# A gated residual block on one core: a third stream of block pairs, operand sums made by transfers, and paced preparation

## The chip, the cores and the metric

One core of a Trainium2 chip runs the kernel. The metric is the device time of one execution in microseconds (us), the median of repeated runs. The engines are TensorE (PE, matrix products), VectorE (DVE), ScalarE (ACT), GpSimd (POOL) and SyncE (SP, which here only issues DMA transfers).

## The reference, cut to what matters

A sequence of S = 512 positions of width D = 1024 goes through one residual block. All matrices are float32.

```python
h = rmsnorm(x, norm_mix_g)
u, v, bg, cg, xs, ga, gb = split(einsum('bsd,dc->bsc', h, w_in))   # seven products 1024 x 1024
u = gelu(u); v = rmsnorm(gelu(v), norm_v_g)
a = spatial_gating(u, v, w_s, b_s)                                # branch A
c = bg * causal_dwconv(cg * xs, conv_w)                           # branch B: three streams bg, cg, xs
m = sigmoid(ga + b_gate_a) * (a @ w_proj_a) + sigmoid(gb + b_gate_b) * (c @ w_proj_b)
x = x + m @ w_out
x = x + relu(rmsnorm(x, norm_ff_g) @ w_ff1) ** 2 @ w_ff2          # 1024 -> 4096 -> 1024
return rmsnorm(x, norm_final_g)
```

## The kernel before

**Products.** Activations stay in SBUF with channels on the 128 partitions and the 512 positions along the row; the weights stream in from HBM, each byte once. To keep float32 accuracy with the faster fp32r matmul, every operand is split into a high part (a cast on ACT, L117, `whi<-raw`) and a low part (a subtraction on DVE, L118, `wlo<-raw,whi`), and every product is three matmuls: high by high, high by low, low by high.

There are two forms of product. A **unit** (`unit_matmuls`, L265 to L267) is one output tile of 128 channels over all 1024 input channels: 8 steps of 3 matmuls of 512 columns. A **block pair** (`block_pair`) makes two such output tiles at once by Strassen's method in Winograd's form: the 2 by 2 blocks are combined by additions, and 7 block products replace 8. One block product (`product`, L283 to L285) is 12 matmuls of 256 columns. The order on PE is P1, P2, then P7 of the pair ahead (kept back in the list `late`), E, P6, then D of the pair ahead, then F. P7 and D of one pair both add into the bank A of that pair, and ACT copies the bank (L313) after P7 and before D may write to it again. `first` and `second` are the functions that turn the two output tiles into the next value.

**Operands.** A pair needs four split operands: `a1` (two blocks), `s31` (two sums of blocks), `s42` (two further sums) and `a22` (one block). The two-block operands rotate through 4 buffers, `a22` has one buffer of its own, which D of the pair ahead must have read first. DVE makes the sums: `add1` (L218, 1024 elements in a row) for s31 and `add2` (L222 and L223, 512 each) for s42.

**Loads.** SP issues one 1 MB transfer for a pair (`raw<-w_pair`, four blocks, L148) or for two units (`raw<-w_main`, L144). There are two raw buffers. The step `load(ld + 2)` stands behind the last split of load `ld`, which for a pair is that of a22, so a load starts when the buffer's last reader on DVE is done.

**Order.** Preparation steps (splits, sums, loads) stand in one list in the order of their use. `pump()` takes one step ahead of every product; `need()` takes steps until the operand at hand is there. The tile framework's scheduler then settles the order on each engine, and each engine runs its own list in that order.

**Stages.** The v product with its own small loads (0 to 31 us of the profiled execution); units of u with the spatial gating `mix` woven in; gate A as 4 pairs with units of the projection of a between them; branch B in four calls of `c_pair`, each two pairs (the streams `c_w` and `x_w`) and then two units (the third stream `b_w`); gate B with its projection; the output projection; and the two feed-forward products, where pairs and units alternate. After `x_first` or `x_second`, `conv` does the three-tap convolution on DVE: the first tap at L616, the others at L618.

## Time and profile before

| | |
|---|---|
| median of 3 runs | 789.09 us (789.01 to 789.1) |
| the profiled execution, its own time | 788.42 us |
| its span in the trace | 786.6 us |
| PE busy in the span | 778.4 us, 99% |
| DVE, ACT, POOL busy | 568.8 us (72%), 365.7 us (46%), 6.3 us (1%) |
| granted TensorE clock, mean | 0.997 |
| moved by DMA | 83.60 MB |

Of the span, the trace gives each instruction's start, its length, and in brackets how long its engine was idle before it and what released it. "whi<-raw" reads as: writes the tile whi from the tile raw. The profiled execution is 0.67 us shorter than the median of the runs, and 1.8 us of it lie outside the span.

### The profile page before, as it was taken

The numbers are of one execution on the slowest core, as the hardware profiler recorded it, in microseconds if no ns is written. First come the engines' busy times: TensorE is split into PE (matmuls) and PEld (weight loads), VectorE is DVE, ScalarE is ACT, GpSimd is POOL, SyncE is SP. The second block draws the span as 40 slices with busy tenths as digits, with TensorE's granted clock in tenths as the row PEclk, the third lists the DMA queues.
The fourth block names the chain that finished last, engine by engine and source line by source line (L and its number), as shares of the span: only waits on it lengthen the run. The fifth ranks groups of instructions, "written<-read, shape, count | busy, mean of one in ns | idle before, by whom it ended". The sixth has DMA issues, their size and how long they took to land.

```text
span 786.6 us, 11560 instructions
## 1 busy us (share of the span) xinstructions
PE 778.4 (99%) x4798; PEld 701.3 (89%) x4798; DVE 568.8 (72%) x854; ACT 365.7 (46%) x548; POOL 6.3 (1%) x14
## 2 busy tenths in 40 slices
PE   9999999999999999999999999999999999999996
PEld 6888899999999999999988999889988999889886
DVE  7849785566889889766769998647955687557644
ACT  8625363444344444444555676324742365226521
POOL 0000000000000000000000000000000000000000
PEclk9999999999999999999999999999999999999998
DMA  9602113331332314332633033330353024311403
GB/s 333 218 40 92 68 55 107 107 107 55 107 115 102 107 62 154 107 108 86 229 114 107 1 107 125 144 107 1 107 182 140 1 91 177 107 54 55 161 1 107
DMA packets 21443, 83.60 MB, mean 106 GB/s; under 512 B 1936, under 2 KB 2960, under 8 KB 17296
## 3 DMA queue, kind: packets, MB, share of 16 engines
q1 hardware_dynamic: 20384, 81.27, 29.5%
q10 hardware_dynamic: 1008, 1.61, 0.6%
q8 instruction: 37, 0.61, 0.3%
q14 instruction: 14, 0.11, 0.0%
HBM read 80.78 MB, written 2.10 MB: 105 GB/s over the span
## 4 chain that ended last, share of the span: by engine, by line
PE 98%; DMA 0%; ACT 0%; DVE 0%; POOLq 0%; DVEq 0%; issue 0%
PE bank L265 17%; PE bank L266 17%; PE bank L267 17%; PE bank L284 14%; PE bank L285 14%; PE bank L283 14%; PE bank L477 6%; PE bank L528 1%; DMA vec<-vecs 0%; PE bank L369 0%; PE st L358 0%; PE bank L747 0%; PE st L793 0%; DVE ob L759 0%; POOLq L929 0%; ACT x L120 0%
## 5 line engine op out<-in xcount | busy, mean ns | idle before, releaser
L117 ACT CAST whi<-raw 128x1024 fp32r<-128x1024 f32 (+1 forms) x136 | 129.0, 950 | 180.4 <-PE bank L266 117.7
L118 DVE TENSOR_TENSOR wlo<-raw,whi 128x1024 fp32r<-128x1024 f32 (+1 forms) x136 | 148.8, 1096 | 18.2 <-ACT whi L117 16.3
L117 ACT CAST whi<-wsum 128x1024 fp32r<-128x1024 f32 x64 | 67.2, 1051 | 80.9 <-PE bank L266 41.3
L265 PE MATMUL bank<-z,whi 128*128 128x512 f32 (+1 forms) x272 | 102.7, 378 | 0.0
L266 PE MATMUL bank<-z,whi 128*128 128x512 f32 (+1 forms) x272 | 102.6, 377 | 0.0
L267 PE MATMUL bank<-z,wlo 128*128 128x512 f32 (+1 forms) x272 | 102.4, 376 | 0.0
L118 DVE TENSOR_TENSOR wlo<-wsum,whi 128x1024 fp32r<-128x1024 f32 x64 | 78.2, 1222 | 21.0 <-ACT whi L117 20.2
L283 PE MATMUL bank<-ft,whi 128*128 128x256 f32 x256 | 72.5, 283 | 0.0
L285 PE MATMUL bank<-xc,wlo 128*128 128x256 f32 x256 | 72.4, 283 | 0.0
L284 PE MATMUL bank<-xc,whi 128*128 128x256 f32 x256 | 72.4, 283 | 0.0
L285 PE MATMUL bank<-ft,wlo 128*128 128x256 f32 x256 | 72.4, 283 | 0.0
L284 PE MATMUL bank<-ft,whi 128*128 128x256 f32 x256 | 72.4, 283 | 0.0
L283 PE MATMUL bank<-xc,whi 128*128 128x256 f32 x256 | 72.3, 282 | 0.0
L860 DVE TENSOR_TENSOR res<-bank,res 128x512 f32<-128x512 f32 x30 | 20.7, 691 | 60.9 <-PE bank L267 60.9
L267 PEld LDWEIGHTS bank<-z,wlo 128*128 128x128 f32 x272 | 51.2, 188 | 9.4
L265 PEld LDWEIGHTS bank<-z,whi 128*128 128x128 f32 x272 | 51.2, 188 | 9.2
L266 PEld LDWEIGHTS bank<-z,whi 128*128 128x128 f32 x272 | 51.2, 188 | 8.9
L284 PE MATMUL bank<-fb,whi 128*128 128x256 f32 x192 | 54.4, 283 | 0.0
L283 PE MATMUL bank<-fb,whi 128*128 128x256 f32 x192 | 54.4, 283 | 0.0
L283 PE MATMUL bank<-x,whi 128*128 128x256 f32 x192 | 54.4, 283 | 0.0
L285 PE MATMUL bank<-x,wlo 128*128 128x256 f32 x192 | 54.3, 283 | 0.0
L284 PE MATMUL bank<-x,whi 128*128 128x256 f32 x192 | 54.3, 283 | 0.0
(157 smaller groups left out, 1797.6 us busy)
## 6 DMA issues: line engine op xcount, KB each, us to landing
raw<-w_main SPq DMA_DIRECT2D x36, 1024.0 KB, 4.9
raw<-w_pair SPq DMA_DIRECT2D x32, 1024.0 KB, 4.8
vraw<-w_v SPq DMA_DIRECT2D x16, 256.0 KB, 5.5
xin<-xT SPq DMA_DIRECT2D x8, 256.0 KB, 5.2
res<-xT SPq DMA_DIRECT2D x8, 256.0 KB, 4.7
out_a<-o SPq DMA_DIRECT2D x4, 256.0 KB, 2.3
wsT<-w_sT ACTq DMA_DIRECT2D x2, 256.0 KB, 4.8
bsb<-b_sb ACTq DMA_DIRECT2D x2, 256.0 KB, 6.0
```

What stands on the lines that cost most here:

```text
L117: nc.scalar.copy(hi, src)
L118: nc.vector.tensor_tensor(lo, src, hi.bitcast(F32), op=ALU.subtract)
L265: nc.tensor.matmul(psum, hi[:, c], act_hi[k][:, cols], start=k == 0, stop=False)
L266: nc.tensor.matmul(psum, hi[:, c], act_lo[k][:, cols], start=False, stop=False)
L267: nc.tensor.matmul(psum, lo[:, c], act_hi[k][:, cols], start=False, stop=k == KT - 1)
L283: nc.tensor.matmul(out, w_hi, x_hi, start=first and sl == 0, stop=False, skip_group_check=True)
L284: nc.tensor.matmul(out, w_hi, x_lo, start=False, stop=False, skip_group_check=True)
L285: nc.tensor.matmul(out, w_lo, x_hi, start=False, stop=sl == KS - 1, skip_group_check=True)
L477: nc.tensor.matmul(vbanks[h][b], xs[k][:, b * P : (b + 1) * P], ws, start=k == 0 and ws is vh and xs is xh, stop=k == KT - 1 and xs is xl,)
L528: nc.tensor.matmul(pm[:, b * P : (b + 1) * P], vt[b][g // 4][:, (g % 4) * P : (g % 4 + 1) * P], wsT[:, g, :], start=True, stop=True,)
L860: nc.vector.tensor_add(res[j], py, res[j])
```

## The change

The third stream of branch B becomes a third block pair in each `c_pair`, with `b_first` and `b_second`; so there are 36 pairs where there were 32, and 32 loads of units where there were 36. The sums of s31 are no longer added on DVE: for each pair, GpSimd issues one transfer that copies two blocks (512 KB, L225 of the new kernel) into a slot, and, when that has landed, one that adds a third block to both (L226, `accum_op`). One such slot exists until the mixing of branch A has ended, three after that. The load of a pair on SP brings three blocks (768 KB) instead of four. The first tap of the convolution goes from DVE to ACT (L649 of the new kernel). `pump()` no longer takes a split whose time, by a model clock `now` that counts products, lies ahead of an assumed landing of its load.

```diff
@@ -135,9 +135,16 @@
     wfree = list(range(N_WBUF))
     a22_busy = [False]
 
+
+
+    now = [0.0]
+    T_PRODUCT, T_HALF, T_RAW, T_SUM = 1.44, 2.72, 7.0, 12.0
+    t_load = {}
+
     def load(n):
         if n >= len(loads) or n in raw_of:
             return
+        t_load[n] = now[0]
         kind, i = loads[n]
         r = raws.tile([P, 4, S], F32, name="raw")
         if kind == "u":
@@ -145,12 +152,12 @@
                 r.rearrange("p (u a) s -> p u (a s)", u=2), w_main[i : i + 2].rearrange("u p f -> p u f")
             )
         else:
-            nc.sync.dma_start(r, w_pair[i])
+            nc.sync.dma_start(r[:, :3, :], w_pair[i, :, :3, :])
         raw_of[n] = r
 
-    def add_operand(src, n=2):
-        o = {"ready": False, "n": n}
+    def add_operand(src, due, n=2):
+
+        o = {"ready": False, "n": n, "due": due}
 
         def step():
             if n == 2:
@@ -181,11 +188,11 @@
 
         while steps and n:
             step, o = steps[0]
-            if o is not None and (not wfree if o["n"] == 2 else a22_busy[0]):
+            if o is not None and ((not wfree if o["n"] == 2 else a22_busy[0]) or o["due"]() > now[0]):
                 return
             steps.pop(0)
             step()
-            n -= 1
+            n -= o is not None
 
     def need(o):
         while not o["ready"]:
@@ -193,16 +200,30 @@
 
     units = []
     pairs = []
+
+    def raw_due(ld):
+        return t_load.get(ld, 1e9) + T_RAW
 
     def plan_units(n):
         for _ in range(n // 2):
             ld = len(loads)
             loads.append(("u", len(units)))
             for e in range(2):
-                units.append(add_operand(lambda ld=ld, e=e: raw_of[ld][:, 2 * e : 2 * e + 2, :]))
+                units.append(add_operand(
+                    lambda ld=ld, e=e: raw_of[ld][:, 2 * e : 2 * e + 2, :], lambda ld=ld: raw_due(ld)
+                ))
             add_step(lambda ld=ld: load(ld + 2))
 
-    sums_t = None
+    s31_free, s31_of, t_build = [], {}, {}
+
+    def build():
+
+        while s31_free and len(t_build) < w_pair.shape[0]:
+            i, s = len(t_build), s31_free.pop(0)
+            s31_of[i] = s
+            t_build[i] = now[0]
+            nc.gpsimd.dma_start(s.t, w_pair[i, :, 1:3, :])
+            nc.gpsimd.dma_start(s.t, w_pair[i, :, 3:4, :].broadcast_to([P, 2, S]), accum_op=ALU.add)
 
     def plan_pair():
         ld = len(loads)
@@ -211,24 +232,28 @@
         def raw(a, b):
             return raw_of[ld][:, a:b, :]
 
-        s31, s42 = sums_t[0].t, sums_t[1].t
-
-        def add1():
-
-            nc.vector.tensor_tensor(s31, raw(1, 3), raw(3, 4).broadcast_to([P, 2, S]), op=ALU.add)
+        n = len(pairs)
+
+        def due():
+            return raw_due(ld)
+
+        def done1():
+            s31_free.append(s31_of.pop(n))
+            build()
 
         def add2():
 
+            s31, s42 = s31_of[n].t, s42_t.t
             nc.vector.tensor_tensor(s42[:, 1, :], s31[:, 1, :], raw(1, 2)[:, 0, :], op=ALU.add)
             nc.vector.tensor_tensor(s42[:, 0, :], s42[:, 1, :], raw(0, 1)[:, 0, :], op=ALU.add)
 
         tl = {}
-        tl["a1"] = add_operand(lambda: raw(0, 2))
-        add_step(add1)
-        tl["s31"] = add_operand(lambda: s31)
+        tl["a1"] = add_operand(lambda: raw(0, 2), due)
+        tl["s31"] = add_operand(lambda: s31_of[n].t, lambda: t_build.get(n, 1e9) + T_SUM)
         add_step(add2)
-        tl["s42"] = add_operand(lambda: s42)
-        tl["a22"] = add_operand(lambda: raw(2, 3), n=1)
+        add_step(done1)
+        tl["s42"] = add_operand(lambda: s42_t.t, due)
+        tl["a22"] = add_operand(lambda: raw(2, 3), due, n=1)
         add_step(lambda: load(ld + 2))
         pairs.append(tl)
 
@@ -255,7 +280,9 @@
                 need(o)
             unit_k(psum, o, k, act_hi, act_lo)
             if k == KT // 2 - 1:
+                now[0] += T_HALF
                 run_late()
+        now[0] += T_HALF
         release(o)
         run_late()
 
@@ -283,6 +310,7 @@
             nc.tensor.matmul(out, w_hi, x_hi, start=first and sl == 0, stop=False, skip_group_check=True)
             nc.tensor.matmul(out, w_hi, x_lo, start=False, stop=False, skip_group_check=True)
             nc.tensor.matmul(out, w_lo, x_hi, start=False, stop=sl == KS - 1, skip_group_check=True)
+        now[0] += T_PRODUCT
         if name in ("P2", "D", "F", "P7"):
             release(o)
 
@@ -378,7 +406,7 @@
             nc.vector.tensor_add(acc, acc, sq)
 
 
-    sums_t = slots(2, "wsum")
+    s42_t = Slot("wsum")
     plan_units(KT)
     for _ in range(KS):
         plan_pair()
@@ -386,7 +414,7 @@
     for _ in range(KS):
         plan_pair()
         plan_pair()
-        plan_units(2)
+        plan_pair()
     for _ in range(KS):
         plan_pair()
         plan_units(2)
@@ -479,6 +507,7 @@
                     start=k == 0 and ws is vh and xs is xh, stop=k == KT - 1 and xs is xl,
                 )
         vp.give()
+        now[0] += T_HALF
         if KT < i <= KT + NB:
             v_sq(0, i - KT - 1)
         if i == KT + 1:
@@ -511,6 +540,8 @@
             nc.vector.tensor_scalar(vt[b][h], vt[b][h], rv[:, b : b + 1], None, op0=ALU.mult)
 
 
+    s31_free.append(Slot("wsum31"))
+    build()
     a_s = []
     us = {}
 
@@ -582,6 +613,8 @@
             for g in range(KT - LAG, KT):
                 mix(g)
             give(*vt_s, *ws_s)
+            s31_free.extend(slots(2, "wsum31"))
+            build()
             ah, al = hi_lo(a_s)
         m1_s.append(Slot(f"m1{p}"))
         pps = []
@@ -613,7 +646,7 @@
             j = j0 + e
             y = temp("y")
             w = [col(V_CONV + 8 * i, j) for i in range(3)]
-            nc.vector.tensor_scalar(y, z[:, 0:S], w[0], None, op0=ALU.mult)
+            nc.scalar.activation(y, z[:, 0:S], AF.Copy, scale=w[0])
             for i in (1, 2):
                 nc.vector.scalar_tensor_tensor(y, z[:, i : S + i], w[i], y, op0=ALU.mult, op1=ALU.add)
             nc.vector.tensor_mul(y, y, R)
@@ -635,13 +668,19 @@
 
         block_pair(next_pair(), right_x, c_first, c_second)
         block_pair(next_pair(), right_x, x_first, x_second)
-        pbs = []
-        for e in range(2):
-            pbs.append(bank())
-            unit_matmuls(pbs[e], xh, xl)
-        for e in range(2):
-            nc.vector.tensor_mul(ys[e], pbs[e], ys[e])
-            split_into(ch[j0 + e], cl[j0 + e], ys[e])
+
+        def b_first(c1):
+            nc.vector.tensor_mul(c1, c1, ys[0])
+            split_into(ch[j0], cl[j0], c1)
+
+        def b_second(n21, c2):
+            y = ys[1]
+            for h, src in ((0, n21), (1, c2[:, N2:])):
+                cs = slice(h * N2, (h + 1) * N2)
+                nc.vector.scalar_tensor_tensor(c2[:, cs], src, -1.0, y[:, cs], op0=ALU.mult, op1=ALU.mult)
+            split_into(ch[j0 + 1], cl[j0 + 1], c2)
+
+        block_pair(next_pair(), right_x, b_first, b_second)
 
     for p in range(KS):
         c_pair(2 * p)
@@ -896,9 +935,9 @@
         return g.reshape(M // 256, P, 4, S)
 
     w_pair = np.concatenate(
-        [blocks(ga_w), np.stack([blocks(c_w), blocks(x_w)], 1).reshape(-1, P, 4, S), blocks(gb_w),
+        [blocks(ga_w), np.stack([blocks(c_w), blocks(x_w), blocks(b_w)], 1).reshape(-1, P, 4, S), blocks(gb_w),
          blocks(f(w_ff1)[0])], 0)
-    seq = [woven(u_w), woven(f(w_proj_a)[0]), woven(b_w), woven(f(w_proj_b)[0])]
+    seq = [woven(u_w), woven(f(w_proj_a)[0]), woven(f(w_proj_b)[0])]
     seq.append(units(f(w_out)[0])[[n // 2 + KS * (n % 2) for n in range(KT)], 0])
     ff2 = units(f(w_ff2)[0])
     for ck in range(NCH):
```

Line numbers in the rows below that come from the new kernel are its own. `DMAHW` in brackets stands for a transfer issued by SP or ACT, `DMASW` for one issued by POOL; the number after a name only tells one tile from another.

**ACT in branch B.** Here `whi<-raw` is the cast of an a1 (1024 elements) or an a22 (512), and `c2<-bank` at L313 (before) or L341 (after) is the copy of bank A after P7, which must end before D writes to that bank. In the middle of the stage, before:

```order
L298 COPY c1_2417<-bank_2414 128x256 [waits PE_49]
L117 CAST whi_2538<-raw_2381 128x1024 [waits DMAHW1_49,PE_49,Activation_49]
L117 CAST whi_2554<-raw_2381 128x1024 [waits PE_49]
L313 COPY c2_2331<-bank_2327 128x256 [waits PE_49]
L303 COPY c2_2418<-bank_2416 128x256 [waits PE_49]
L305 COPY c1_2417<-bank_2414 128x256 [waits PE_49]
L117 CAST whi_2510<-raw_2252 128x512 [waits PE_49]
```

After:

```order
L326 COPY c1_2165<-bank_2162 128x256 [waits PE_49]
L117 CAST whi_2297<-raw_2167 128x1024 [waits DMAHW6_49,PE_49,Activation_49]
L341 COPY c2_2043<-bank_2039 128x256 [waits PE_49]
L117 CAST whi_2314<-wsum311_1037 128x1024 [waits DMASW3_49]
L331 COPY c2_2166<-bank_2164 128x256 [waits PE_49]
L333 COPY c1_2165<-bank_2162 128x256 [waits PE_49]
L117 CAST whi_2265<-raw_2044 128x512 [waits DVE_49,PE_49]
```

Before, the load whose casts stand ahead of the copy is one of units, every third of the stage; after, it is that of the next pair, at each of some ten pairs in a row, and the cast of the s31 that follows the copy waits for a transfer of POOL.

**POOL at the start**, where `r4<-ms4,expo` makes the reciprocal root that the first norm needs. Before:

```order
L73 MEMSET expo_90 128x4
L351 TENSOR_TENSOR r4_336<-ms4_334,expo_90 128x4 [waits DVE_49,Pool_49]
L351 TENSOR_TENSOR r4_546<-ms4_544,expo_90 128x4 [waits DVE_49,Activation_49,Pool_49]
L351 TENSOR_TENSOR r4_4214<-ms4_4212,expo_90 128x4 [waits DVE_49,Pool_49]
```

After:

```order
L73 MEMSET expo_90 128x4
L225 DMA wsum31_559<-w_pair 128x1024 [waits DMAHW2_49,DMAHW1_49,DVE_49]
L226 DMA wsum31_559<-w_pair 128x2x512 [waits DMASW0_49]
L379 TENSOR_TENSOR r4_335<-ms4_333,expo_90 128x4 [waits DVE_49,Pool_49]
L379 TENSOR_TENSOR r4_549<-ms4_547,expo_90 128x4 [waits DVE_49,Activation_49,Pool_49]
L225 DMA wsum31_559<-w_pair 128x1024 [waits DMASW1_49,DVE_49]
L226 DMA wsum31_559<-w_pair 128x2x512 [waits DMASW2_49]
L225 DMA wsum310_1036<-w_pair 128x1024 [waits PE_49]
```

The first sum's two transfers now stand ahead of `r4` on POOL's list, and its adding transfer waits there for its copying one.

**DVE while the mixing ends and the operands of the second pair are made.** `t_m` and `t_u` are values of the mixing, `t_u<-bank` frees a bank for PE. Before:

```order
L118 TENSOR_TENSOR wlo_826<-wsum0_103,whi_825 128x1024 [waits Activation_49]
L533 SCALAR_TENSOR_TENSOR t_m_818<-bank_813,vec_76,bsb_376 128x512 [waits PE_49]
L218 TENSOR_TENSOR wsum0_103<-raw_921 128x1024 [waits DMAHW3_49,DVE_49]
L537 TENSOR_TENSOR t_m_818<-t_m_818,t_u_689 128x512 [waits DVE_49]
L118 TENSOR_TENSOR a2_821<-t_m_818,a2_821 128x512 [waits Activation_49]
L521 TENSOR_TENSOR t_u_855<-bank_824,R_537 128x512 [waits PE_49]
L118 TENSOR_TENSOR wlo_871<-wsum1_104,whi_870 128x1024 [waits Activation_49]
L533 SCALAR_TENSOR_TENSOR t_m_863<-bank_858,vec_76,bsb_376 128x512 [waits PE_49]
L222 TENSOR_TENSOR wsum1_104<-wsum0_103,raw_921 128x512 [waits DVE_49]
L537 TENSOR_TENSOR t_m_863<-t_m_863,t_u_721 128x512 [waits DVE_49]
```

After:

```order
L118 TENSOR_TENSOR wlo_827<-wsum31_559,whi_826 128x1024 [waits Activation_49]
L564 SCALAR_TENSOR_TENSOR t_m_819<-bank_814,vec_76,bsb_375 128x512 [waits PE_49]
L568 TENSOR_TENSOR t_m_819<-t_m_819,t_u_691 128x512 [waits DVE_49]
L118 TENSOR_TENSOR a2_822<-t_m_819,a2_822 128x512 [waits Activation_49]
L552 TENSOR_TENSOR t_u_858<-bank_825,R_540 128x512 [waits PE_49]
L118 TENSOR_TENSOR wlo_874<-wsum_103,whi_873 128x1024 [waits Activation_49]
L564 SCALAR_TENSOR_TENSOR t_m_866<-bank_861,vec_76,bsb_375 128x512 [waits PE_49]
L247 TENSOR_TENSOR wsum_103<-wsum31_559,raw_924 128x512 [waits DMAHW3_49,DMASW3_49,DVE_49]
L568 TENSOR_TENSOR t_m_866<-t_m_866,t_u_723 128x512 [waits DVE_49]
```

The DVE sum `wsum0` of the second pair is gone, and the first half of its s42 (`wsum_103<-wsum31`) now waits on DVE for both transfers of POOL (DMASW3), with the mixing behind it.

## Rows read from the trace of the kernel before

**Rows 1.** The page, part 1: busy time of each engine.

```profile
PE 778.4 (99%) x4798; PEld 701.3 (89%) x4798; DVE 568.8 (72%) x854; ACT 365.7 (46%) x548; POOL 6.3 (1%) x14
```

**Rows 2.** Waits of PE: who for whom, us in total, times, longest.

```profile
PE st L78 <- DVE warm L65: 1.0, 1, 1.0
PE bank L477 <- ACT vp L117: 0.8, 1, 0.8
```

**Rows 3.** Timeline of PE in branch B: start, length, what.

```profile
201.76 0.28 PE L283 MATMUL bank<-x,whi 128*128 128x256 f32 x1
...
203.20 0.40 PE L265 MATMUL bank<-x,whi 128*128 128x512 f32 x1
...
205.94 0.28 PE L283 MATMUL bank<-xc,whi 128*128 128x256 f32 x1
```

**Rows 4.** Busy time by window: A:B, length, PE, PEld, DVE, ACT, POOL, clock.

```profile
core 0: us, PE busy (x) PEld busy (x) DVE busy (x) ACT busy (x) POOL busy (x), PEclk, DMA share, GB/s
...
455.00:475.00 20.00, 20.00 (x169) 20.00 (x169) 18.77 (x30) 15.03 (x25) 0.00 (x0) 1.00 0.30 107
...
230.10:261.20 31.10, 31.10 (x219) 29.16 (x218) 27.67 (x43) 13.48 (x20) 0.00 (x0) 1.00 0.30 102
```

**Rows 5.** Timeline of DVE in branch B.

```profile
234.96 0.69 DVE L625 TENSOR_TENSOR z<-c,c 128x512 f32<-128x512 f32 x1
235.68 0.49 DVE L616 TENSOR_SCALAR y<-z,vec 128x512 f32<-128x512 f32 x1
236.09 1.22 DVE L218 TENSOR_TENSOR wsum<-raw 128x1024 f32<-128x1024 f32 x1
237.23 0.75 DVE L618 SCALAR_TENSOR_TENSOR y<-z,vec,y 128x512 f32<-128x512 f32 x1
...
240.83 0.69 DVE L619 TENSOR_TENSOR y<-y,R 128x512 f32<-128x512 f32 x1
241.43 0.42 DVE L314 TENSOR_TENSOR c<-c 128x256 f32<-128x256 f32 x1
241.76 0.69 DVE L643 TENSOR_TENSOR y<-bank,y 128x512 f32<-128x512 f32 x1
```

**Rows 6.** Timeline of SP, ACT and DVE around one load in branch B.

```profile
230.96 3.68 SPq L148 DMA_DIRECT2D raw<-w_pair  x2
...
232.94 0.62 ACT L117 CAST whi<-raw 128x512 fp32r<-128x512 f32 x1 [0.95 <-PE bank L284]
235.79 1.06 ACT L117 CAST whi<-raw 128x1024 fp32r<-128x1024 f32 x1 [2.23 <-DMA raw<-w_pair]
...
239.51 0.36 ACT L313 COPY c<-bank 128x256 f32<-128x256 f32 x1
```

**Rows 7.** The page, part 6: issues, KB each, median us to landing.

```profile
raw<-w_pair SPq DMA_DIRECT2D x32, 1024.0 KB, 4.8
vraw<-w_v SPq DMA_DIRECT2D x16, 256.0 KB, 5.5
```

**Rows 8.** The page, part 2: GB/s in 40 slices of the span.

```profile
GB/s 333 218 40 92 68 55 107 107 107 55 107 115 102 107 62 154 107 108 86 229 114 107 1 107 125 144 107 1 107 182 140 1 91 177 107 54 55 161 1 107
```

**Rows 9.** Timeline of all engines at the start.

```profile
17.43 1.89 DVE L118 TENSOR_TENSOR vp<-vraw,vp 128x512 fp32r<-128x512 f32 x3
...
25.40 1.06 ACT L117 CAST whi<-raw 128x1024 fp32r<-128x1024 f32 x1 [0.71 <-DMA raw<-w_main]
...
28.27 8.01 PE L477 MATMUL bank<-vp,x 128*128 128x512 f32 x34
28.45 0.16 DVE L349 TENSOR_SCALAR ms<-st 128x4 f32<-128x4 f32 x1 [0.73 <-PE st L358]
28.77 1.02 POOL L351 TENSOR_TENSOR r<-ms,expo 128x4 f32<-128x4 f32 x1 [27.28 <-DVE ms L349]
29.82 0.69 ACT L440 ACTIVATE vt<-bank,r 128x512 f32<-128x512 f32 x1 [1.39 <-POOL r L351]
```

**Rows 10.** Timeline of DVE while the second pair's operands are made.

```profile
86.61 1.23 DVE L118 TENSOR_TENSOR wlo<-wsum,whi 128x1024 fp32r<-128x1024 f32 x1 [0.16 <-ACT whi L117]
...
94.81 0.68 DVE L222 TENSOR_TENSOR wsum<-wsum,raw 128x512 f32<-128x512 f32 x1
...
98.45 0.69 DVE L521 TENSOR_TENSOR t_u<-bank,R 128x512 f32<-128x512 f32 x1 [0.97 <-PE bank L267]
99.30 1.23 DVE L118 TENSOR_TENSOR wlo<-raw,whi 128x1024 fp32r<-128x1024 f32 x1 [0.16 <-ACT whi L117]
```

## Prediction

> **What bounds the kernel now.** I read the busy times first: PE works 778.4 us of a span of 786.6, DVE 568.8 [rows 1]. Then the list of what PE waits for: two entries, 1.8 us in all, both ahead of 8 us [rows 2]; from there to 770 us the list is empty. So every microsecond of PE work that goes is worth a microsecond, as long as no new wait of PE takes its place, and nothing that becomes lighter on another engine is worth anything by itself. PE's clock is at its upper level of 2.4 GHz throughout (granted 1.00 in the windows of [rows 4]). The whole question is therefore: how much PE work goes, and which of the new waits reach PE.
>
> **What goes on PE.** In branch B a block product of 12 matmuls of 256 columns takes 203.20 − 201.76 = 1.44 us, and the 12 matmuls of 512 columns behind it 205.94 − 203.20 = 2.74 us [rows 3]. A `c_pair` before is two pairs and two units: 14 products, 20.16 us, and 48 matmuls of 512 columns, 10.94 us (31.10 less 20.16; four times 2.74 gives 10.96), together the 31.10 us of the window [rows 4]. After, it is three pairs: 21 × 1.44 = 30.24 us. The gain is 0.86 us in each of four calls, **3.44 us**. With no new wait the profiled execution of 788.42 us would become 784.98; the median of the runs lies 0.67 above the profiled one, which makes 785.65. That is the floor.
>
> **What it costs DVE and ACT in branch B.** Durations on DVE overlap a little, so I take start to start: 1024 elements 237.23 − 236.09 = 1.14, 512 elements 241.43 − 240.83 = 0.60, 256 elements 0.33, the convolution's first tap 236.09 − 235.68 = 0.41 [rows 5]. Out of a `c_pair` go two `add1` (2.28), the low parts of two units (2.28) and two first taps (0.82): 5.38. In come the third pair's low parts (three of 1024 and one of 512, 4.02), its `add2` (1.20) and about 1.06 more of evacuation: 6.28. So 27.67 us of DVE in 31.10 [rows 4] become about 28.6 in 30.24, 94.6% where it was 89%. There is a precedent: between 455 and 475 us DVE is busy 18.77 of 20 us, 94%, and PE stays at 20.00 [rows 4]. ACT goes to some 18 of 30.24. Neither is a bound by its sum; I cost both at nothing, and what hides them is the operands' lead of a product or more. If that lead is gone, DVE's lag goes onto the loop below.
>
> **The start.** The first sum's slot is free once DVE has the second of the three low parts that start at 17.43 [rows 9], near 19 us. POOL's two transfers then run beside SP's load of raw weights that lands at 25.40 (the cast that waits for it starts then) [rows 9]. In the first slice of the span 333 GB/s are moved [rows 8]; at that rate the 512 KB of the copy take 0.524 MB / 333 = 1.57 us of all engines, and I bound the adding transfer by the same again. The load could land 1.57 to 3.1 us later. Behind it stand two low parts on DVE, then `ms`, then POOL's root, then the first gelu, which frees a bank. DVE had 0.73 us idle ahead of `ms`; the gelu ends at 30.51, and PE, from 28.27, needs that bank 11 matmuls later by its order, 28.27 + 11 × 0.228 = 30.78 [rows 9]: 0.27 more. Cover 1.0 us. So the stall is 0 (the load keeps its place), 1.57 − 1.0 = 0.57, or 3.1 − 1.0 = 2.1. The memset of wsT, now behind more of DVE's list, waits for its own load and can take the same 0.73 us. I take **0.25**, nearest to the first two, since the copy has six microseconds before the load is wanted. POOL's root is queued behind the adding transfer on POOL; that transfer is issued near 25 us, 3.8 us ahead of the root's 28.77, so I cost that at nothing.
>
> **The second pair's sum.** There is one slot until the mixing ends. It comes free when DVE has the low part of the first pair's sum, 86.61 + 1.23 = 87.84 [rows 10]. Two transfers in a row, each at 4.8 us for 1 MB [rows 7], would put the sum at 97.4; at 3 us each at 93.8. In the order after, the first half of the second pair's s42 waits for it on DVE at the place where `wsum<-wsum,raw` began at 94.81 [rows 10], and the mixing's `t_m`, its next `t_u` (98.45) and a low part (99.30) are behind it. The delay on DVE is 0 to 2.6, or 3.5 if the adding transfer is slower than a load of 1 MB. DVE has 0.97 idle ahead of `t_u` [rows 10], and PE has an operand in hand, so only a part gets through: bounds 0 and 3.5, taken **0.6**. That no row shows an adding transfer at all is the largest unknown of the case. By the Trainium skill (DMA: Bandwidth & Descriptors, Anatomy of one DMA — SWDGE path), a transfer issued by GpSimd costs 2.0 us and its bytes at 436 GB/s; for 512 KB I estimate 3.2 us, two of them 6.4 us, which would put this sum at 94.2, ahead of its use, make this term zero and the time 0.6 lower. No run here shows that yet.
>
> **The loop in branch B.** With three pairs in a row, each load depends on the product D: D of a pair ends, a22 of the next is cast (its one buffer was D's), DVE makes the low part, SP issues the load two ahead into that raw buffer, the load lands, ACT casts its a1, and behind that cast on ACT stands the copy of bank A that the next D waits for (the order section shows these rows). Before, the same chain is seen once per `c_pair`: cast 232.94, next issue 230.96 + 3.68 − 0.33 = 234.31, 1.37 us later [rows 6]; and the load issued at 230.96 lets its cast start at 235.79, 4.83 us [rows 6]. Its copy came 239.51, and nobody waited [rows 2]. Priced: D 1.45, cast to issue 1.37, the a1 cast 1.05, copy 0.37, hand-overs 0.10, together 4.34, plus T, the load, plus L, any lag on DVE or ACT. A pair takes 7 × 1.44 = 10.08, so the loop is free while T + L is below **5.74**. T for 768 KB alone is about 4.83 − 0.262 MB / 333 = 4.04; with a copy of POOL in the same engines 1.57 more, 5.6. L is 0 (ACT and DVE at once) to 1.6 (one 1024-element low part of 1.14 and one of 0.60 ahead). So T + L runs from 4.0 to 7.2: per pair nothing, or up to 1.46 us. The transfers of POOL are there for 2 × 3 to 2 × 4.9 us of every 10, so about half of the loads meet one. I take an excess of 0.06 at 12 pairs, **0.7**, with bounds 0 and 14.6.
>
> **The other parts.** Gate A, gate B and the first feed-forward product keep their alternation of pair and units, so a load there still has the time of both, and the sums have three slots. DVE loses 36.5 us (32 × 1.14) of `add1` over the whole kernel, which bounds nothing, DVE being busy 72% of the span [rows 1]; cost zero. The first tap on ACT adds 8 × 0.62, hidden by ACT's 13.48 of 31.10 [rows 4].
>
> **Sum.** −3.44 + 0.25 + 0.6 + 0.7 = −1.89 on the profiled time of 788.42: 786.5, and on the median **787.2 us**.
>
> **Rivals.** *The sums come late and eat the gain* (within 0.2%): the start costs 0.57, the second pair's sum 2, the loop 0.7, together 3.3 against 3.44: 789.0 at the median, 788.7 with a little less at the start. For it: the adding transfer must read its target as well as write it, and no row bounds it from above. Against: only two places, each with cover. A small part of it is that the change does not do what it says, because the scheduler sets other waits.
>
> *The loop in branch B becomes the bound* (slower): T + L exceeds 5.74 by 0.5 us at 10 pairs, 5 us, with 0.85 at start and sum: 789.09 − 3.44 + 5.85 = 791.5, up to 800 at the upper bound. It decides from T = 5.74 with no lag on DVE, or from T = 4.1 with a lag of 1.6. For it: the margin between 5.6 and 5.74 is nearly nothing, and DVE at 94% makes lag likely. Against: 256 KB loads at the start, issued close together, take 5.5 [rows 7], in the busiest stretch of the trace, so even crowded loads land below 5.74. A rule speaks for it: transfers issued from several engines run on the same 16 DMA engines and interleave (the Trainium skill, DMA: Bandwidth & Descriptors, Issuing engines are not separate DMA queues), so POOL's 1 MB of writes per pair would lengthen every load that it meets; by the row of 4.83 alone, without it, the loop would be free.
>
> **How the numbers follow.** Forecast 0.42 (785.6 to 787.5), no measurable change 0.30 (787.5 to 790.7), slower 0.28 (above). A measurement of this kernel tells about 0.2%, 1.6 us, from no change. The forecast's own range is 785.6 to 787.5. The range that should hold 8 times in 10 begins at the floor, 785.6, and reaches into the slower case up to 792.5, an excess of about 0.6 us at 10 pairs.
>
> **What would show it.** Right: no wait of PE in branch B, `c_pair` at 30.24 us, the waits of PE a few tenths near 31 us and one near 95 to 105. The loop as rival shows as PE waiting for ACT's copy of bank A ahead of D, with ACT waiting for `raw<-w_pair` just before, and `c_pair` above 31.1. Late sums show as DVE's or ACT's waits for POOL's transfers with PE waiting behind. Wrong altogether would be a wait of PE at a place named nowhere here, such as gate B or the first feed-forward product, where I cost the new transfers at nothing.

## The result and the profile after

The changed kernel takes 812.78 us (811.49 to 815.17), the kernel before 789.05: a ratio of 1.0307 (1.0288 to 1.0326). The profiled execution took 811.49 us, with a span of 809.7 where it was 786.6: 23.1 us longer. Its time is 26.5 us above the floor of the prediction (784.98).

The waits of PE, which were two lines before [rows 2], are now these (us in total, times, longest):

```profile
PE bank L310 <- ACT c L341: 11.7, 11, 1.7
PE bank L310 <- ACT c L331: 3.9, 5, 1.6
PE bank L505 <- ACT vt L468: 3.8, 1, 3.8
PE st L78 <- DVE warm L65: 1.0, 1, 1.0
PE bank L505 <- ACT vp L117: 0.5, 1, 0.5
PE bank L312 <- DVE wlo L118: 0.4, 1, 0.4
```

The first is what the loop in branch B was to look like: PE, ahead of D (L310), waits for ACT's copy of bank A (L341); eight of its eleven waits, 10.5 us, lie in branch B. In the second PE waits ahead of F for ACT's copy of bank E (L331); 3.1 of its 3.9 us lie in the feed-forward products. The third is the start. The page's parts on DMA answer to [rows 7]:

```profile
q1 hardware_dynamic: 19872, 71.83, 25.3%
q0 software_dynamic: 14976, 37.75, 21.0%
...
wsum<-w_pair POOLq DMA_DIRECT2D x72, 512.0 KB, 5.3
raw<-w_main SPq DMA_DIRECT2D x32, 1024.0 KB, 5.2
raw<-w_pair SPq DMA_DIRECT2D x36, 768.0 KB, 4.3
```

q0 is POOL's queue: half of SP's bytes, but 21.0% of the engines' time against SP's 25.3%. The medians look harmless; the stage decides.

**Where the time went.** I took the same product of both programs at the stage boundaries and subtracted its start before from its start after. What each stage adds to the distance (on PE the v product ends at 50.18 us of the trace before, later than the 31 us given for it above):

| stage | predicted | measured |
|---|---|---|
| start, to the end of the v product | +0.25 | +5.83 |
| units of u, mixing, second pair's sum | +0.6 | +0.64 |
| rest of gate A | 0 | 0.00 |
| branch B (with the gain of 3.44) | −3.44 + 0.7 | −3.44 + 13.24 |
| gate B, output projection | 0 | 0.00 |
| feed-forward products, four chunks | 0 | +3.73, +1.44, +1.33, +0.03 |

Together 22.8 of the 23.1 us. In branch B a wait costs some 0.26 us more than its length: the turn with the wait of 1.39 took 11.73 us instead of 10.08.

**The loop in branch B.** One turn, from ACT, DVE, SP and PE's timelines:

```profile
228.53 0.62 ACT L117 CAST whi<-raw 128x512 fp32r<-128x512 f32 x1 [0.69 <-PE bank L311]
...
228.18 1.22 DVE L118 TENSOR_TENSOR wlo<-wsum,whi 128x1024 fp32r<-128x1024 f32 x1
229.32 0.68 DVE L248 TENSOR_TENSOR wsum<-wsum,raw 128x512 f32<-128x512 f32 x1
229.92 0.42 DVE L680 SCALAR_TENSOR_TENSOR c<-bank,y 128x256 f32<-128x256 f32 x1
230.25 0.68 DVE L118 TENSOR_TENSOR wlo<-raw,whi 128x512 fp32r<-128x512 f32 x1
...
230.97 0.33 SPq L155 DMA_DIRECT2D raw<-w_pair  x1
...
237.24 0.69 DVE L247 TENSOR_TENSOR wsum<-wsum,raw 128x512 f32<-128x512 f32 x1 [3.30 <-DMA raw<-w_pair]
237.22 1.04 ACT L117 CAST whi<-raw 128x1024 fp32r<-128x1024 f32 x1 [5.00 <-PE bank L312]
238.17 0.37 ACT L341 COPY c<-bank 128x256 f32<-128x256 f32 x1
...
238.59 0.39 PE L310 MATMUL bank<-xc,whi 128*128 128x256 f32 x1 [1.39 <-ACT c L341]
```

The a22 is cast at 228.53 (its buffer is free when D has read it); DVE makes its low part only at 230.25, behind a low part and a sum that had themselves waited for the load before; SP issues at 230.97; the load lands and its a1 is cast at 237.22, 6.25 us later (the row names PE, long done by then; DVE's row at 237.24 names the load, the later of the two); behind that the copy, and then D. From cast to issue it is 2.44 us where [rows 6] had 1.37 (1.37 in the first two turns of the row, 2.4 to 2.9 in the eight from here on). Over the stage (205 to 318 us) the raw tile's view has, for loads of 768 KB:

```profile
DMA to landing us min/median/max: 4.0/5.8/6.6
```

Before, it was 4.7, 4.9 and 5.5 for loads of 1 MB. What runs beside them stands on POOL's timeline:

```profile
229.70 0.60 POOL L225 DMA_DIRECT2D wsum<-w_pair  x1 [5.44 <-DVE wlo L118]
235.06 1.17 POOL L226 DMA_DIRECT2D wsum<-w_pair  x1 [4.76 <-DMA wsum<-w_pair]
241.57 0.60 POOL L225 DMA_DIRECT2D wsum<-w_pair  x1 [5.34 <-DVE wlo L118]
```

The copy starts at 229.70, the load at 230.97; the next pair is 241.57 and 242.57. The copy is released by DVE's low part of s31, which ends at 229.40, the load by that of the a22, which ends at 230.93: two steps of the same pair that stand close together on DVE. So the copy doesn't meet half of the loads. In this row it starts 1.0 to 1.8 us ahead of nine loads of ten, and these land in 5.1 to 6.6 us. Only the first load's copy starts earlier, 3.1 us ahead of it, and that load lands in 4.0.

### The profile page after: what moved, and what is told of

Read it like the earlier page. It is cut to its first block, busy times and chain, and to the rows that moved or that the text cites. A ratio compares the mean times of both kernels' runs of the same rounds, so it can differ in the third digit from the quotient of the medians.

```text
span 809.7 us, 12032 instructions
## 1 busy us (share of the span) xinstructions
PE 781.6 (97%) x4942; PEld 707.3 (87%) x4942; DVE 543.1 (67%) x846; ACT 377.1 (47%) x580; POOL 69.8 (9%) x86
## 3 DMA queue, kind: packets, MB, share of 16 engines
q1 hardware_dynamic: 19872, 71.83, 25.3%
## 4 chain that ended last, share of the span: by engine, by line
PE 70%; DMA 15%; DVE 8%; issue 3%; ACT 3%; POOL 0%; DVEq 0%; POOLq 0%; ACTq 0%
PE bank L292 14%; PE bank L293 14%; PE bank L294 13%; DMA raw<-w_pair 9%; PE bank L310 8%; PE bank L311 8%; PE bank L312 8%; PE bank L505 4%; DMA raw<-w_main 4%; DVE wlo L118 4%; ACT whi L117 2%; DMA wsT<-w_sT 1%; DVE wsum L248 1%; DVE wsum L247 1%; DMA wsum<-w_pair 1%
## 5 line engine op out<-in xcount | busy, mean ns | idle before, releaser
L118 DVE TENSOR_TENSOR wlo<-raw,whi 128x1024 fp32r<-128x1024 f32 (+1 forms) x136 | 145.9, 1079 | 20.9 <-ACT whi L117 19.9
L117 ACT CAST whi<-wsum 128x1024 fp32r<-128x1024 f32 x72 | 75.6, 1050 | 68.8 <-PE bank L293 41.9
L310 PE MATMUL bank<-xc,whi 128*128 128x256 f32 x320 | 91.3, 285 | 10.5 <-ACT c L341 10.5
L118 DVE TENSOR_TENSOR wlo<-wsum,whi 128x1024 fp32r<-128x1024 f32 x72 | 87.9, 1221 | 18.1 <-ACT whi L117 17.3
L311 PE MATMUL bank<-xc,whi 128*128 128x256 f32 x320 | 90.5, 283 | 0.0
L312 PE MATMUL bank<-xc,wlo 128*128 128x256 f32 x320 | 90.5, 283 | 0.0
L310 PE MATMUL bank<-ft,whi 128*128 128x256 f32 x256 | 72.8, 284 | 1.2 <-ACT c L341 1.2
L310 PEld LDWEIGHTS bank<-xc,whi 128*128 128x128 f32 x320 | 61.3, 191 | 12.8 <-ACT c L341 12.1
L310 PE MATMUL bank<-x,whi 128*128 128x256 f32 x240 | 68.2, 284 | 0.8 <-ACT c L331 0.8
L312 PE MATMUL bank<-x,wlo 128*128 128x256 f32 x240 | 67.9, 283 | 0.0
L311 PE MATMUL bank<-x,whi 128*128 128x256 f32 x240 | 67.9, 283 | 0.0
L311 PEld LDWEIGHTS bank<-xc,whi 128*128 128x128 f32 x320 | 61.3, 192 | 0.6
L312 PEld LDWEIGHTS bank<-xc,wlo 128*128 128x128 f32 x320 | 61.3, 192 | 0.0
L293 PEld LDWEIGHTS bank<-z,whi 128*128 128x128 f32 x272 | 51.2, 188 | 9.0
```

The source lines that it names most:

```text
L117: nc.scalar.copy(hi, src)
L118: nc.vector.tensor_tensor(lo, src, hi.bitcast(F32), op=ALU.subtract)
L293: nc.tensor.matmul(psum, hi[:, c], act_lo[k][:, cols], start=False, stop=False)
L310: nc.tensor.matmul(out, w_hi, x_hi, start=first and sl == 0, stop=False, skip_group_check=True)
L311: nc.tensor.matmul(out, w_hi, x_lo, start=False, stop=False, skip_group_check=True)
L312: nc.tensor.matmul(out, w_lo, x_hi, start=False, stop=sl == KS - 1, skip_group_check=True)
```

## The experiments

The landing of loads and PE's stage distances below are read as above. Theory A: POOL's transfers make SP's loads late, and the loop of loads passes that on. B: three pairs in a row are too much for DVE and ACT. C: the pacing holds steps back.

**e1, third stream by units again** (one part undone).

```diff
-        plan_pair(); plan_pair(); plan_pair()
+        plan_pair(); plan_pair(); plan_units(2)
...
-        block_pair(next_pair(), right_x, b_first, b_second)
+        (the two units of the kernel before)
```

> The changed kernel with one part undone: branch B's third stream again by units (32 pairs, units woven in), the sums of s31 still by POOL's transfers, pacing and first tap as changed. Theory A (POOL's transfers lengthen SP's loads and that breaks the loop of loads): the stalls of the changed kernel outside branch B stay, +5.8 at the start, +0.6 at the second pair's sum, +6.5 in the first feed-forward product, and branch B goes to 31.1 to 32 us a call; time 802 to 805. Theory B (three pairs in a row are too much for DVE and ACT, whatever the transfers): branch B 31.1 and the feed-forward stalls, which are no part of it, stay as well, 802. Theory C (pacing holds steps back): as A. If the feed-forward stalls go, all three are wrong there.

797.11 us. Start +3.27, second pair +0.79, branch B 0.00, feed-forward +3.9. So branch B stalls only with three pairs in a row, but the feed-forward product, whose pairs the change doesn't touch, stalls without them. Its size, 3.9 for 6.5, and the start's, 3.3 for 5.8, were not as expected. The loads of pairs in branch B land in 3.9 to 4.6 us here, with no copy started just ahead of them, so this run does not separate the row of three pairs from the lateness of the loads; e5 and e12 do.

**e2, sums on DVE again, no transfers of POOL.**

```diff
-        nc.sync.dma_start(r[:, :3, :], w_pair[i, :, :3, :])
+        nc.sync.dma_start(r, w_pair[i])
...
+        def add1():
+            nc.vector.tensor_tensor(s31_t.t, raw(1, 3), raw(3, 4).broadcast_to([P, 2, S]), op=ALU.add)
```

> The changed kernel with POOL's transfers undone: s31 is summed by DVE's add1 again, a pair's load is 1 MB again; the third pair, pacing and the tap on ACT stay. Theory A: loads land in 4.8 us again, no stall in the first feed-forward product (now +6.5), start below +2; branch B bound by DVE, 28.6 + 3 x 1.14 = 32.0 us a call in place of 33.5, or less; time 788 to 796. Theory B: branch B stays at 33.5 or above, since DVE has more work, not less; feed-forward stalls stay; time 805 or more. Theory C (pacing): start, branch B and feed-forward stalls all stay, 805 to 812.

792.0 us. Start −0.06, feed-forward 0.00; branch B with gate B +2.6, that is 6.0 short of the gain, with DVE busy 112.27 of 117 us. Loads of 1 MB land in 4.7 to 5.0 us. B would have made it worse, since DVE has more to do: B falls as the cause of the 13 us, though a DVE at 96% does cost: PE's waits there are now mostly for casts and low parts of the operands themselves (L301 <- ACT whi, L303 <- DVE wlo).

**e3, the adding transfer left out.**

```diff
-            nc.gpsimd.dma_start(s.t, w_pair[i, :, 3:4, :].broadcast_to([P, 2, S]), accum_op=ALU.add)
```

> The changed kernel without the adding transfer: the sum s31 lacks its second summand, so half of POOL's transfers are gone; everything else is as changed. Theory A by traffic alone: half of POOL's bytes, so about half of the 26 us that were lost, 798 to 801. Theory A by the adding transfer being dearer than a copy (POOL's 37.75 MB took 21.0% of the engines' time, SP's 71.83 MB 25.3%): more than two thirds of it goes, 790 to 796. Theories B and C: nothing changes, 810 to 813.

The sums then lack their second summand. 809.36 us: both sizes missed, only 3 us went. Loads in branch B still land in 5.1 / 5.8 / 6.3 us (min, median, max), because it is the copy that starts beside them: POOL's 238.39, SP's 239.39. The traffic as such is not what is paid for; 13.6% of the engines' time there, in place of 42.3%, left branch B at +15.0 against the floor, where the changed kernel has +13.2.

**e4, no pacing.**

```diff
-            if o is not None and ((not wfree if o["n"] == 2 else a22_busy[0]) or o["due"]() > now[0]):
+            if o is not None and (not wfree if o["n"] == 2 else a22_busy[0]):
```

> The changed kernel without pacing: a split is taken as soon as a buffer is free, as before; third pair and POOL's transfers stay. Theory C (pacing holds splits back and so loads): the stalls shrink by 10 us or more, below 803. Theories A and B: within 4 us of the changed kernel, 809 to 817, or slower, since a cast that waits for its transfer then stands further ahead on ACT.

812.71 us, stage by stage within 2 us of the changed kernel. C falls.

**e5, the loop loosened by a second a22 buffer and an earlier load.**

```diff
-            s31_free.extend(slots(2, "wsum31"))
+            s31_free.extend(slots(1, "wsum31"))
+            a22_free.append(Slot("w22b", F32R))
...
+            add_step(add2)              # from the third pair on: ahead of s31 and s42
+            a22_and_load()
```

> The changed kernel with the loop of loads loosened: a second buffer for a22 (in place of the third slot for s31), and from the third pair on a22 is split and the next load issued ahead of the splits of s31 and s42, so that a load hangs on the D of two pairs before. POOL's transfers stay as they are. Theory A1 (a copy of POOL that starts with SP's load makes it land late, and the loop from D over the load to the next D passes that on): branch B 30.24 to 31 us a call in place of 33.5, no stall in the first feed-forward product, start still +3 to +6; time 790 to 796, although loads land as late as before. Theory A2 (the transfers cost time by themselves, by slowing what DVE and ACT do or by holding all engines): 806 to 813.

791.61 us. Branch B −3.45, feed-forward +0.2, with the same transfers and loads as late. The start kept its +6.2, the second pair +0.8. A1 holds, A2 falls.

**e6, copies held until the next load has landed.**

```diff
+                nc.gpsimd.tensor_tensor(g4, raw(0, 1)[:, 0, :NB], expo, op=ALU.add)
+                build()
```

> The changed kernel with POOL's copies moved in time: from the fourth sum on, a tiny operation of POOL that reads the next load's landed tile stands ahead of the copy on POOL, so that a copy starts when SP's load has landed and not with it. Theory A1: loads without a copy beside them land in 4.0 to 4.5 us in place of 5.6 to 6.2, branch B 30.3 to 31.5 a call unless the adding transfer meets the load in its place; time 792 to 802. Theory A2: the same bytes in the same time, 808 to 813. If the adding transfers meet the loads and these land in 5 us or more, the time says nothing of A1 and the loads' landing does.

814.07 us (809.63 to 818.5), a miss: the edit did not move the copies. Loads in branch B still land in 5.8 us (median), and POOL's timeline has

```profile
226.28 0.73 POOL L248 TENSOR_TENSOR g<-raw,expo 128x4 f32<-128x4 f32 x1 [0.64 <-DMA raw<-w_pair]
230.93 0.61 POOL L225 DMA_DIRECT2D wsum<-w_pair  x1 [3.91 <-DVE wlo L118]
```

The tiny operation is over four microseconds before the copy, which waits for its slot as before, and SP's load follows at 232.22. The copies start 1.0 to 2.0 us ahead of the loads, as in the changed kernel. So this run tells nothing of A1 or A2.

**e7, sums by GpSimd itself.**

```diff
+            nc.gpsimd.tensor_tensor(s31_t.t, raw(1, 3), raw(3, 4).broadcast_to([P, 2, S]), op=ALU.add)
```

> The changed kernel with the sums of s31 neither by transfers nor on DVE: GpSimd adds them from the landed 1 MB load (tensor_tensor, 1024 elements). No extra transfers, DVE at 28.6 us of 30.24 a call. Theory A (transfers are the cause, 1 or 2): no stall at the start or in the feed-forward product, branch B 30.24 to 31, time 785.6 to 789, if GpSimd's add takes under 4 us and doesn't slow DVE. Theory B (three pairs in a row are too much for DVE at 94%): branch B at 31.5 or above, as in the run with DVE's sums, 791 or more.

809.18 us, a miss. Start +0.08, branch B 18.1 short of the gain, feed-forward +5.7, with loads at 4.8 us. The sum takes 2.4 to 3.25 us and stands between the load's landing and the rest; DVE waits for it, and DVE's own work is stretched while it runs. The timelines of POOL and DVE:

```profile
268.03 2.41 POOL L233 TENSOR_TENSOR wsum<-raw 128x1024 f32<-128x1024 f32 x1 [9.06 <-DMA raw<-w_pair]
...
270.47 0.69 DVE L238 TENSOR_TENSOR wsum<-wsum,raw 128x512 f32<-128x512 f32 x1 [2.70 <-POOL wsum L233]
...
279.38 2.65 POOL L233 TENSOR_TENSOR wsum<-raw 128x1024 f32<-128x1024 f32 x1 [8.94 <-DMA raw<-w_pair]
...
279.68 2.63 DVE L333 TENSOR_TENSOR c<-c 128x256 f32<-128x256 f32 x1
```

The last row's instruction took 0.42 before [rows 5]. So the stalls came back without one late load, on another path: PE's waits in branch B are mostly ahead of L303, for DVE's low parts, and none is for the copy of bank A. That GpSimd's sum causes them is read from these rows and was not tested apart. Two falls of the granted clock (from 248.2 and 292.6 us) are part of the 18.1.

**e8, e5 and the first two sums on DVE.**

```diff
+            b = 4 if i < 2 else 3
+            nc.sync.dma_start(r[:, :b, :], w_pair[i, :, :b, :])
...
-    s31_free.append(Slot("wsum31"))
-    build()
+    s31_of[0] = s31_of[1] = Slot("wsum31")      # taken at the start
```

> The loosened loop of e5, and the first two pairs' sums made by DVE's add1 from a 1 MB load, so that no POOL transfer runs before the mixing has ended (34 sums by transfers). Theory A1, term by term: the start's +6.2 and the second pair's +0.8 of e5 go, branch B keeps its gain of 3.44 and the feed-forward product its +0.2; time 785.7 to 786.5, faster than the kernel before by 0.3 to 0.4%. If the start's loss came from something else in the change (the later load of wsT, pacing), it stays, 791.

**785.47 us** (785.38 to 785.92), a ratio of 0.9958 (0.9945 to 0.9972) to the kernel before, which took 788.81 beside it: 0.4% faster, with the interval clear of 1. Start −0.01, second pair 0, branch B −3.44, feed-forward +0.15. PE's waits are two lines again:

```profile
PE st L78 <- DVE warm L65: 1.0, 1, 1.0
PE bank L531 <- ACT vp L121: 0.2, 1, 0.2
```

The prediction's floor, 785.65, is reached.

**e9, the first build held back to 58 us.**

```diff
+    nc.gpsimd.tensor_tensor(s31_free[0].t[:, 0, :NB], R[:, :NB], expo, op=ALU.add)
     build()
```

> The changed kernel with its first build held back alone: a tiny operation of POOL writes the first sum's slot from the tile R, which exists at some 57 us, so that the first copy starts behind that. Theory: the start's +5.8 goes to below 0.3, although wsT's load is still ordered behind bsb's and its memset ahead of the raw splits on DVE; second pair's sum, branch B and the feed-forward product stay as in the changed kernel; time 806 to 808. If the order of wsT is what costs, the start stays at +3 to +6.

812.01 us. The start keeps +4.62 with no transfer of POOL before 58 us: my theory of the start falls for the larger part. Of the 4.62, 0.51 lies ahead of 28.3 us; behind it PE waits 2.19 and the granted clock falls once (from 34.1 us). What is left is in DVE's timeline:

```profile
28.56 0.48 DVE L520 MEMSET wsT<- 64x512 f32 x1 [3.66 <-DMA wsT<-w_sT]
29.08 2.36 DVE L118 TENSOR_TENSOR wlo<-raw,whi 128x1024 fp32r<-128x1024 f32 x2
31.36 0.16 DVE L377 TENSOR_SCALAR ms<-st 128x4 f32<-128x4 f32 x1
```

The memset waits for wsT's load, and two low parts and `ms` behind it. In the kernel before, wsT's load is issued at 16.2 and lands in 4.8 us; here it is issued at 20.0 and takes 7.1 to 7.9. In the combination, e8, where `ms` is at 28.45, it is issued at 15.9.

**e10, the kernel before with idle copies (31 in the trace).**

```diff
+            if extra_s:
+                nc.gpsimd.tensor_tensor(extra_s[0].t[:, 0, :NB], s42[:, 0, :NB], expo, op=ALU.add)
+                nc.gpsimd.dma_start(extra_s[0].t, w_pair[len(pairs) - 1, :, 1:3, :])
```

> The kernel before with POOL's traffic alone added: from the third pair on, 30 copies of 512 KB of weights into a slot that nobody reads, each started behind add2 of a pair; sums, loads and streams as before. Theory A1 (a copy beside a load makes it late, and rows of pairs have no margin for it): loads of pairs land in 5.8 us or more, branch B stays at 31.1 a call (its loop is broken by units), the first feed-forward product, four pairs in a row, loses 3 to 8 us; time 792 to 797. If the first feed-forward product loses nothing, the margin there was wide and the changed kernel's 6.5 us come from the new order on DVE and ACT.

790.25 us, below what was expected. Branch B 0.00, loads there 4.7 / 5.0 / 6.1 us; the feed-forward product loses 1.1, all of it in its first chunk (another 0.6 lies in the v product, ahead of the first copy, and is none of theirs). So 512 KB beside loads cost little by themselves, in the old order of steps and with the copy at another point of the turn: four of the copies in branch B start 0.33 us behind a load and not ahead of it, and there the load takes 4.9 to 5.1 us, once 6.1, and the copy 5.9 to 6.8.

**e11, the first sum's slot taken at the start.**

```diff
     s42_t = Slot("wsum")
+    first_s31 = Slot("wsum31")
...
+            nc.gpsimd.tensor_tensor(first_s31.t[:, 0, :NB], acc[:, :NB], expo, op=ALU.add)
```

> The changed kernel with one thing moved: the first sum's slot is taken at the very start, as the kernel before took its second sum slot, so that wsT and bsb get the slots that they had before (in the program's order wsT's load is ahead of bsb's again, its memset in the old place); the first copy still starts near 20.6 us, since a tiny operation of POOL that reads the finished sum of squares stands ahead of it. Theory S (the slots' numbering moved wsT's load 3.5 us later, and its memset on DVE holds the splits and the norm): start below +0.6. Theory A at the start (POOL's transfers make the loads late): start stays at +3 or more, wsT's landing at 7 us or more though it is issued at 16 us. Branch B and the feed-forward product stay as in the changed kernel either way; time 806 to 808 by S, 811 or more by A.

812.66 us; start +2.06, of which 0.53 lies ahead of 28.3 us, so between the two. wsT is issued at 16.26 and lands in 4.6 us, its memset at 21.64: S holds for the larger part. The rest is POOL's queue:

```profile
21.88 0.75 POOL L225 DMA_DIRECT2D wsum<-w_pair  x1 [0.34 <-POOL wsum L515]
...
28.98 0.16 DVE L377 TENSOR_SCALAR ms<-st 128x4 f32<-128x4 f32 x1 [1.07 <-PE st L386]
29.77 1.22 POOL L226 DMA_DIRECT2D wsum<-w_pair  x1 [7.14 <-DMA wsum<-w_pair]
30.53 1.53 POOL L379 TENSOR_TENSOR r<-ms,expo 128x4 f32<-128x4 f32 x1
```

The copy takes 7.6 us to land beside the start's loads, the adding transfer waits for it on POOL, and the root, ready at 29.14, waits behind that until 30.53; PE waits 1.2. The feed-forward and branch B losses stayed. They even grew, from 13.2 to 16.7 us (with the beginning of gate B) and from 6.5 to 8.1: the granted clock fell three more times, at 235.5, 331.1 and 505.2 us, each time behind a wait of PE. That hides in the total what the start gained.

**e12, the second a22 buffer alone.**

```diff
-            s31_free.extend(slots(2, "wsum31"))
+            s31_free.extend(slots(1, "wsum31"))
+            a22_free.append(Slot("w22b", F32R))
```

> The changed kernel with a second buffer for a22 (in place of the third slot for s31) and nothing else: the order of the steps stays, a22 and the next load still come behind s31, s42 and their buffers. If the loop runs through a22's single buffer alone, branch B goes to 30.3 to 31 us a call as in e5, time 791 to 795. If it also runs through the four buffers that s31 and s42 wait for, ahead of a22 in the list of steps, branch B stays above 32, 800 to 812.

791.5 us. Branch B −3.44 to the hundredth (a pair every 10.08 us, 208.07 to 218.15), feed-forward +0.15, and the loads land as late as in the changed kernel, 4.7 / 5.7 / 7.1 us (216 to 310 us, the longest a load of units). PE's waits are

```profile
PE bank L512 <- ACT vt L475: 4.2, 1, 4.2
PE st L78 <- DVE warm L65: 1.0, 1, 1.0
PE bank L512 <- ACT vp L121: 0.5, 1, 0.5
PE bank L317 <- ACT c L338: 0.3, 1, 0.3
```

The first is the start, the last the second pair; none is in branch B. The copies still start 1.0 to 2.3 us ahead of the loads, so the sum slot that was given up is not what changed. One buffer, D's, closed the loop.

## Why the prediction was wrong, step by step

- **What goes on PE:** right. Wherever the loop is open (e5, e8, e12) branch B is 3.44 us shorter.
- **The start, 0.25:** wrong in its step, not only in its size. I priced the contention of POOL's copy with SP's raw load and gave the memset of wsT at most 0.73 us. The change of slots (one sum slot at the start for two) gave wsT another slot, so its load is issued near 20 us and not at 16.2, and DVE, in order, stands for it; e11, with the slot back, issues it at 16.26. I named the memset's later place on DVE and did not price the load it waits for. With no transfer at all PE waits 2.19 us for this (e9). In the runs with POOL's transfers as well, wsT's second load lands in 8.4 to 9.9 us (7.9 in e9), and PE waits 2.69 to 4.19. Their loss is 3.2 to 6.7 us; the 3.2 and 3.3 (e3, e1) are the two runs whose granted clock did not fall behind the wait. POOL's queue, which I cost at nothing, cost nothing in the changed kernel, where the root begins at 32.86, right behind `ms` (32.55 to 32.71); once wsT is back in its place it is worth 1.2 (e11).
- **The second pair's sum, 0.6:** right, 0.64 (0.5 to 0.8 in the other runs with both transfers, 0 in e3 without the adding one). The mechanism is as written: DVE stood 2.82 us at `wsum<-wsum,raw` (103.55), within the bounds of 0 to 3.5, and part of it reached PE. That the part was so near 0.6 is luck, since no row gave it. The estimate of 6.4 us for the two transfers, which would have made the term zero, failed: they took 9.5 (93.97 to 103.47).
- **The loop, 0.7 of 0 to 14.6:** the mechanism and the bound were right, the choice wrong. T + L had to stay under 5.74 and I put T at 4.04 to 5.6 and L at 0 to 1.6. T is 5.8 (median), above my upper end. L is set by the loop itself: once a load is late, the low part and the sum that wait for it fall into the gap between D and the a22, and cast to issue goes from 1.37 to 2.4 to 2.9, so that L is 1.0 to 1.5. Two judgements failed: that a copy meets about half of the loads (both are released by neighbouring steps of the same pair, so it meets nearly each), and that 5.5 us of the 256 KB loads was evidence of margin, with 5.74 as the edge. The rival that I named for this was the result; I gave it 0.28 and a price of 5 us for 13.2.
- **The feed-forward product, 0:** wrong as a reading. I wrote that pairs and units alternate there; in the trace before, the first chunk begins with five pairs in a row (F of a pair at 455.66, 465.74, 475.82 and 485.90, one every 10.08 us), the second and third with four and the last with three, as branch B after. I even took a window out of them as my precedent [rows 4], at 94% of DVE, and did not see that it was the same loop running with T = 4.9. With late loads it lost 6.5 us, most of PE's waits now being for the copy of bank E, which stands on ACT behind the cast of a late load (a load of units issued at 495.68 was cast at 502.75, and F waited 1.6); with a second a22 buffer 0.15. The new order with DVE's sums and no transfers cost nothing there (e2, 0.00), so in the changed kernel the loss comes with the transfers. What the order adds to them is open: the copies alone cost 1.1 in the old order (e10) and 4.0 in the new one (e3).
- **Pacing, tap on ACT, the other stages:** nothing, as cost (e4 for pacing; e8, which keeps both, reaches the floor; gates A and B 0.00).

## What to carry to other kernels

Follow a buffer round: write down who frees it, what that starts and who needs the result before it can be freed again, and compare the whole turn with the period. Two transfers released by neighbouring steps of one turn can meet in every turn, so a price for "now and then" must not be used without looking at what releases each. Before adding work to a stage that has a tight turn, look for its single buffer: here one more buffer of 4 KB a partition, in place of a third sum slot, gave back 13 us in branch B and 6 behind it, and only then was the smaller PE work worth its 3.44.

## What the runs showed of the hardware that I had not expected

**A wait of PE can cost its clock too.** After the wait of 3.84 us at the start the granted clock fell from its upper level, 2.4 GHz, to half of it, 1.2, for 3.4 us (35.4 to 38.8). From 28.3 us to the end of the v product it was 27.66 us where it had been 21.91: 5.76 more, 3.84 of them the wait. Of the other 1.9, some 0.3 come with a wait that leaves the clock alone (3.35 for a wait of 3.04 in e1, 3.00 for 2.69 in e3), so the fall cost some 1.6, by this estimate. Windows of the changed kernel (A:B, length, PE, PEld, DVE, ACT, POOL, clock, DMA share, GB/s):

```profile
31.00:35.00 4.00, 0.16 (x2) 0.02 (x1) 3.06 (x6) 1.11 (x3) 1.35 (x1) 1.00 1.07 243
35.00:37.00 2.00, 2.00 (x6) 1.58 (x7) 2.00 (x8) 2.00 (x4) 0.00 (x0) 0.60 0.72 291
37.00:39.00 2.00, 2.00 (x7) 1.59 (x6) 2.00 (x7) 2.00 (x4) 0.00 (x0) 0.54 0.00 0
39.00:41.00 2.00, 2.00 (x10) 1.65 (x9) 2.00 (x6) 1.69 (x4) 0.00 (x0) 1.00 0.00 0
```

The waits of 0.9 to 1.7 us in branch B of the changed kernel, and that of 1.2 at the start of e11, left it at 1.00. But in e11 waits of 1.83, 2.05 and 1.95 us further on were each followed by a fall; around the first of them e11 has

```profile
233.50:235.40 1.90, 0.07 (x2) 0.06 (x1) 1.37 (x3) 1.43 (x3) 0.00 (x0) 1.00 0.97 166
235.60:238.90 3.30, 3.30 (x17) 3.30 (x17) 3.30 (x7) 1.80 (x4) 0.57 (x1) 0.50 0.27 48
```

The waits of 3.04 in e1 and 2.69 in e3 were not followed by one. So the length of a wait alone does not tell it.

**An adding transfer costs the DMA engines more than a copy of its size.** In branch B (218 to 320 us) copies alone took 13.6% for 4.22 MB (e3), copies and additions 42.3% for 9.31 MB: with copies at the first rate, the additions took 27% for 4.65 MB, an estimate of 1.8 times as much per byte. A copy of 512 KB landed 4.0 us (median of 36 in the changed kernel) after its issue, an addition 5.9. By the formula of the Trainium skill (DMA: Bandwidth & Descriptors, Anatomy of one DMA — SWDGE path) I estimated 6.4 us for the two. These runs do not show it, not even for the second pair's sum, with no load of SP under way: 3.82 for the copy, 5.39 for the addition, 9.5 from the first issue to the last landing.

**GpSimd beside DVE:** in e7 a DVE addition of 256 elements with both operands in SBUF stood for 2.63 us, as long as GpSimd's sum beside it (2.65), where it takes 0.42. Six such additions (L333) in branch B start while a sum runs: three of them stood for 2.60 to 2.63 us, and the other three took 0.41, beside sums that took 3.0 to 3.2 us instead of 2.4 to 2.7. The Trainium skill (SBUF — State Buffer, Who interferes with whom) says that a DVE instruction with two SBUF inputs contends with a GpSimd instruction that reads SBUF, and that the order of issue decides which of the two blocks. The rows agree that they contend, and that now the one and now the other is held; the order of issue itself no row shows.
